# A two-layer conditioned transformer with routed experts, then a delta-rule block: where modulation, sums and paired weights are loaded

## The chip, the core and the metric

The kernel runs on one core of a Trainium2 chip, all in fp32. The metric is device time in microseconds (us) of one execution. Times come from runs of the whole kernel, the trace from one profiled execution.

## What is computed

Two layers of a first block are followed by one layer of a second block, on 512 tokens of width 1024 with 256 context tokens beside them in the first layer:

```python
mods = silu(c) @ ada_w[i] + ada_b[i]        # 6 x 1024: shift, scale, gate, twice; cmods from c_ctx
h = rms_norm(x, n1) * (1 + sc1) + sh1       # hc alike for the context
p = h @ w_in                                # 2304 columns: conv a, conv b, window and global attention
x_new = x + g1 * (concat(ya, yb, yc, yd) @ w_out)
h2 = rms_norm(x_new, n2) * (1 + sc2) + sh2
x_new = x_new + g2 * expert_choice_ffn(h2)  # 16 experts; each takes its best 64 tokens (32 of the context)
```

An expert computes `silu(xs @ w_gate) * (xs @ w_up) @ w_down` with three 1024 x 1024 matrices and adds its rows, times their gates, back to the tokens that it took. The second block (gated delta rule, dilated attention, a gated FFN) is not touched.

## The kernel before, in words

PE is TensorE, DVE VectorE, ACT ScalarE, POOL GpSimd; SP issues most loads. The program is written as one stream; a planner orders each engine's instructions by program order and a model of their times, so an instruction may stand earlier on its engine than in the program.

**Entry** (L213 to L399). SP loads the inputs: small parameter rows into `rows` (row_load, L223; five kinds of them on POOL's queue), four tiles of x, the first four 512-column blocks of layer 0's modulation weights (ada_load, L191: four loads of 512 KB a block), two tiles of context, and the first units of w_in (pre0). Blocks 0 and 1 are shift 1, blocks 2 and 3 scale 1. Each x tile is transposed by PE (L369), copied by ACT and scaled by DVE (L372). ada_gen (L309) multiplies a block with silu(c) (L318), copies the sums out (L323), transposes them (L327) and adds the bias on DVE (L329, L330). When all four blocks are done, norm1_first (L386) makes the eight 128-row blocks of the normalised input, as a rounded part `hh` (ACT, L396) and its rest `hl` (DVE L397, L398; POOL for the context). `dx` (L621, L622) stores the transposed x to DRAM and frees its place for the attention tiles; `tabl` (L638) loads the rotation tables there.

**Mixers and output product** (layer, L602). dense (L421) takes unit after unit of 128 output columns: a load of 512 KB into one of five `raw` tiles (raw_tile, L187), a split into `wh` (ACT, L442) and `wl` (POOL, L443), 24 matmuls over eight k blocks (L473, context L475), and an `ev` function. A unit of q gathers 64 + 64 columns from two places with two loads (colload2, L490), one unit for each j. Attention (L537), a 31-tap convolution (L773) and, in layer 0, modulation blocks 4 to 11 of layer 0 and 0 to 7 of layer 1 are woven into the dense steps (L943 to L947). The modulation loads use the same raw tiles. Then the output product runs with the router's logits (L974).

**Router and experts** (experts, L1022). Softmax and top-k run mainly on DVE (L1095 to L1180); the normalised tokens go to DRAM (`hd`, L1132), and gather (L1204) fetches an expert's tokens with an indirect DMA on POOL. wload (L1042) loads weight tiles of 512 KB in order of use: g0, u0, then for each expert g, d of the one before, u. In layer 0 the tiles are 18 `rawA`, five `raw` and two `rawB`; each product step (run_gu L1255, down L1324) pops one tile, multiplies it (L1243, context L1248; layer 1 L1237) and issues the next load. In layer 0, modulation blocks 8 to 11 of layer 1 are loaded through raw tiles ahead of the experts (L1061) and computed within the router's steps (L1090, L1120, L1150). There too, POOL clears a tile (L1136) and SP writes it over the sums (L1138). Experts add their output to `sumx` and `sumc` in DRAM with indirect DMAs (add_rows, L1299); near the end the sums come back through two tiles `rb` (sums_load L1305, after experts 13 and 14's up product), and PE and DVE turn and add them in twelve steps (sums_add, L1310): four within expert 15's up product, eight within its down product. The last experts' rows go through one-hot matmuls (scatter_x L1389, scatter_c L1417), with the squares of the new x for the next norm (L1401 to L1403).

```python
if 3 < b < 11 or (l == 1 and b != 7 and b < 11):       # L320, in ada_gen: prefetch the next block
    ada_load(l, b + 1, hfs=range(4 if l == 1 and b > 7 else 3))
run_all((dense_part(gd, 12), 12))                       # L943: the first four units
for e in range(17): ...                                 # L1443: g(e), down(e - 1), u(e), gather(e + 2)
```

## Time and profile before

| | us |
|---|---|
| runs | 2647.95, 2650.71, 2651.56 (median 2650.71) |
| profiled execution | 2657.17 |
| its span, first to last instruction | 2655.0 |
| its mean granted TensorE clock | 0.971 |

Layer 0's mixers and output product run from about 65 to 460 us, its router to 500, its experts to 1058; layer 1's mixers begin at 1083, its experts run from 1389 to 1860; the rest is the second block. A row of a timeline gives start, duration, engine, line, operation, tiles and, in brackets, how long the engine was idle before it and what ended that. "SPq" and "POOL ... DMA" rows are the issue of a transfer, not the transfer. A row with a count (x8) merges neighbours.

### The profile page before, as it was taken

The numbers are of one execution on the slowest core, as the hardware profiler recorded it, in microseconds if no ns is written. First come the engines' busy times: TensorE is split into PE (matmuls) and PEld (weight loads), VectorE is DVE, ScalarE is ACT, GpSimd is POOL, SyncE is SP. The second block draws the span as 40 slices with busy tenths as digits, with TensorE's granted clock in tenths as the row PEclk, the third lists the DMA queues.
The fourth block names the chain that finished last, engine by engine and source line by source line (L and its number), as shares of the span: only waits on it lengthen the run. The fifth ranks groups of instructions, "written<-read, shape, count | busy, mean of one in ns | idle before, by whom it ended". The sixth has DMA issues, their size and how long they took to land.

```text
span 2655.0 us, 41308 instructions
## 1 busy us (share of the span) xinstructions
PE 2476.4 (93%) x16415; PEld 1500.4 (57%) x16415; DVE 1092.9 (41%) x2371; ACT 870.2 (33%) x1769; POOL 637.8 (24%) x552
## 2 busy tenths in 40 slices
PE   7999999699999999899979989898899999999998
PEld 4766777344444333577753322132577787888886
DVE  4488852311111113689641102021665555444411
ACT  4544362211111110464531111110562435443422
POOL 3533112011111100633220000000333233444443
PEclk8999999899999999799989999999899999999999
DMA  8454455999999998222179999999421102333332
GB/s 281 140 165 139 149 177 197 322 383 385 385 386 385 388 394 313 58 59 52 61 289 386 394 398 399 399 404 409 130 67 32 40 25 64 95 96 96 92 96 67
DMA packets 324758, 584.08 MB, mean 220 GB/s; under 512 B 36864, under 2 KB 190007, under 8 KB 323927
## 3 DMA queue, kind: packets, MB, share of 16 engines
q1 hardware_dynamic: 311943, 555.16, 57.7%
q0 software_dynamic: 12480, 26.23, 4.1%
q8 instruction: 129, 2.11, 0.3%
q14 instruction: 62, 0.51, 0.1%
q10 hardware_dynamic: 144, 0.08, 0.0%
HBM read 556.74 MB, written 18.87 MB: 217 GB/s over the span
## 4 chain that ended last, share of the span: by engine, by line
PE 62%; DMA 21%; DVE 9%; issue 3%; POOL 2%; ACT 1%; SPq 1%; ACTq 0%; DVEq 0%; POOLq 0%
PE px L473 21%; DMA rawA<-in_w_gate_dram 4%; DMA rawA<-in_w_down_dram 4%; PE ax L1243 3%; DMA rawA<-in_w_up_dram 3%; PE yx L1243 3%; PE ux L1243 3%; PE g L473 2%; PE s L553 2%; PE y L584 2%; PE px L475 2%; DMA rawB<-in_w_gate_dram 2%; PE pt L565 2%; PE ac L1248 2%; PE pt L473 2%
## 5 line engine op out<-in xcount | busy, mean ns | idle before, releaser
L443 POOL TENSOR_TENSOR wl<-raw,wh 128x512 fp32r<-128x512 f32 (+1 forms) x312 | 408.2, 1311 | 962.0 <-ACT wh L442 768.1
L442 ACT ACTIVATE wh<-raw 128x512 fp32r<-128x512 f32 (+1 forms) x312 | 193.6, 625 | 441.2 <-PE px L473 211.0
L473 PE MATMUL px<-hh,wh 128*128 128x512 f32 x768 | 315.7, 412 | 6.4 <-DVE xT L1401 1.8
L473 PE MATMUL px<-hh,wl 128*128 128x512 f32 x768 | 313.1, 408 | 6.6 <-POOL wl L443 6.6
L473 PE MATMUL px<-hl,wh 128*128 128x512 f32 x768 | 314.6, 410 | 3.8 <-DVE hl L1019 1.9
L1225 ACT ACTIVATE xt<-tr,mod,a 128x64 f32<-128x64 f32 x256 | 86.9, 405 | 295.5 <-PE tr L1221 285.1
L473 PEld LDWEIGHTS px<-hh,wh 128*128 128x128 f32 x768 | 148.7, 194 | 41.2 <-issue 6.1
L473 PEld LDWEIGHTS px<-hh,wl 128*128 128x128 f32 x768 | 148.8, 194 | 39.7 <-POOL wl L443 7.3
L473 PEld LDWEIGHTS px<-hl,wh 128*128 128x128 f32 x768 | 148.7, 194 | 37.5 <-issue 3.8
L1369 DVE SCALAR_TENSOR_TENSOR Yx<-yx,gcol,Yx 64x512 fp32r<-64x512 f32 x36 | 27.0, 750 | 268.7 <-ACT Yx L1368 268.7
L1209 POOL DMA_INDIRECT xg<-hd,gidx x32 | 29.7, 927 | 431.9 <-PE tr L1221 398.3
L785 DVE SCALAR_TENSOR_TENSOR yT<-ub,cols,yT 128x512 f32<-128x512 f32 (+1 forms) x180 | 126.5, 718 | 0.6
L1243 PE MATMUL ax<-rawA,xt 128*32 128x512 f32 x856 | 116.8, 597 | 2.2 <-DMA rawA<-in_w_gate_dram 2.1
L1273 ACT ACTIVATE sa<-ax 128x512 f32<-128x512 f32 x32 | 19.1, 597 | 290.9 <-PE ax L1243 183.1
L1300 POOL DMA_INDIRECT sumx<-ys,place x14 | 22.0, 1571 | 376.5 <-ACT ys L1347 376.5
L1243 PE MATMUL ux<-rawA,xt 128*32 128x512 f32 x800 | 106.1, 594 | 0.1
L1237 PE MATMUL ux<-rawA,xt 128*64 128x512 f32 x328 | 87.3, 611 | 8.1 <-DMA rawA<-in_w_up_dram 8.0
L1237 PE MATMUL yx<-rawA,hT 128*64 128x512 f32 x316 | 81.5, 621 | 11.0 <-DMA rawA<-in_w_down_dram 10.0
L565 PE MATMUL pt<-tab,P 128*128 128x128 f32 x448 | 82.2, 284 | 6.8 <-DVE PT L571 4.3
L1368 ACT ACTIVATE Yx<-yx,gcol 64x512 fp32r<-64x512 f32 x36 | 24.6, 682 | 190.7 <-PE yx L1237 138.4
L1228 DVE TENSOR_SCALAR xt<-tr,a,mod 128x32 f32<-128x32 f32 x128 | 39.0, 310 | 115.0 <-ACT xt L1225 114.5
L1237 PE MATMUL ax<-rawA,xt 128*64 128x512 f32 x316 | 77.7, 612 | 7.6 <-DMA rawA<-in_w_gate_dram 7.2
(593 smaller groups left out, 4895.0 us busy)
## 6 DMA issues: line engine op xcount, KB each, us to landing
rawA<-in_w_gate_dram SPq DMA_DIRECT2D x186, 512.0 KB, 10.4
rawA<-in_w_up_dram SPq DMA_DIRECT2D x182, 512.0 KB, 10.2
rawA<-in_w_down_dram SPq DMA_DIRECT2D x151, 512.0 KB, 10.4
raw<-in_ada_w_dram SPq DMA_DIRECT2D x80, 512.0 KB, 5.7
raw<-in_w_down_dram SPq DMA_DIRECT2D x74, 512.0 KB, 10.2
raw<-in_w_gate_dram SPq DMA_DIRECT2D x62, 512.0 KB, 8.1
raw<-in_w_in_dram SPq DMA_DIRECT2D x56, 512.0 KB, 3.9
raw<-in_w_up_dram SPq DMA_DIRECT2D x55, 512.0 KB, 10.2
```

The source lines that it names most:

```text
L442: A.activation(wh[:, :n], raw[i][:, a:a + n], AF.Copy)
L443: G.tensor_tensor(wl[:, :n], raw[i][:, a:a + n], wh[:, :n].bitcast(F32), op=OP.subtract)
L473: T.matmul(px, lhsT=w[:, k % 4, :], rhs=h[:, k0 + k, 0:512], start=st, stop=sp_)
L475: T.matmul(pc, lhsT=w[:, k % 4, :], rhs=h[:, k0 + k, 512:nt], start=st, stop=sp_)
L553: T.matmul(s[:, :w], lhsT=q, rhs=k, start=(a == 0), stop=(a == len(mm) - 1))
L565: T.transpose(pt[:, (t - a) * 128:(t - a + 1) * 128], P[:, t * 128:(t + 1) * 128], ident)
L584: T.matmul(y[64 * g:64 * g + 64, bi * 128:(bi + 1) * 128], lhsT=vs[g][t], rhs=PTs[i, g][t // 4][:, (t % 4) * 128:(t % 4 + 1) * 128], start ...
L785: V.scalar_tensor_tensor(acc[:, j, o:o + n], src, w, acc[:, j, o:o + n], op0=OP.mult, op1=OP.add)
L1225: A.activation(xt[:, kk, 0:64], p[:, k * NX:k * NX + 64], AF.Identity, bias=M[l][:, 24 + kk, 0:1], scale=a2[:, kk, 0:1])
L1237: T.matmul(px[64 * g:64 * g + 64, :], lhsT=lx(u), rhs=w[:, 512 * hf:512 * hf + 512], start=first, stop=last)
L1243: T.matmul(px[32 * g:32 * g + 32, :], lhsT=lx(u)[:, 32 * (g % 2):32 * (g % 2) + 32], rhs=w[:, 512 * hf:512 * hf + 512], start=first, stop= ...
L1248: T.matmul(pc[32 * g:32 * g + 32, :], lhsT=lc(u), rhs=w[:, 256 * q:256 * q + 256], start=first, stop=last)
```

## The change

- The entry loads all of x first, then modulation blocks 0 and 2, the context, the first unit of w_in, blocks 1 and 3, and the first q pair; small rows follow, all on SP, and `rows` lies in a raw tile. `pre0[2]` is loaded too.
- Blocks 0 and 2 alone are computed ahead of the first four blocks of the normalised input; blocks 1 and 3 come after the first half of the first dense unit. The three remaining transposes of rows move behind the first unit.
- A q pair's two units share two loads of 512 KB with 256 columns each (pair_load).
- Layer 1's modulation blocks 8 to 11 become 16 more units at the end of layer 0's list of expert loads, in `rawA` tiles, and are computed step by step within scatter_x.
- The sums are cleared beside the output product, from part of `lg`.
- The sums are added back one product earlier: the context's in expert 14's up product (loaded after expert 12's), four steps in expert 15's up product, four in its down product.
- Within the loop over experts SP's instructions keep the order of the program, in both layers.

```diff
@@ tiles and entry @@
-    dx = pool(ctx, "dx", space=DRAM).tile([128, 8 * 768], F32)
+    dxp = pool(ctx, "dx", space=DRAM)
+    dx = dxp.tile([128, 8 * 768], F32)
+    accs = dxp.tile([1024, 512], F32, name="sumx"), dxp.tile([1024, 256], F32, name="sumc")
...
-    rows = ent.tile([128, 4, 128], F32)
+    rows = raw_tile()[:, 0:512].rearrange("p (g c) -> p g c", g=4)
...
-    ada0 = ent.tile([128, 4, 4, 1024], F32)
+    entry2 = ExitStack()
+    ada0 = {b: pl.tile([128, 4, 1024], F32, name=f"ada{b}")
+            for pl, bs in ((ent, (1, 3)), (pool(entry2, "ent2", side="right"), (0, 2))) for b in bs}
...
-    x_load(1)
-    row_load(G, 0, "qn", I["q_norm_g"], 2, dup=True)
-    row_load(G, 0, "kn", I["k_norm_g"], 2, dup=True)
-    row_load(G, 0, "cbb", I["conv_b_b"].rearrange("l (h p) -> (l h) p", p=128), 4)
...
+    for t in range(1, 4):
+        x_load(t)
+    ada_load(0, 0, ada0[0])
+    ada_load(0, 2, ada0[2])
+    for t in range(2):
+        SY.dma_start(cin[:, t, :], I["ctx"][0, t * 128:(t + 1) * 128, :])
+    pre0 = {0: raw_tile().rearrange("p (k c) -> p k c", k=8)}
+    SY.dma_start(pre0[0], I["w_in"][0, :, 1536:1664].rearrange("(k p) c -> p k c", p=128))
+    ada_load(0, 1, ada0[1])
+    ada_load(0, 3, ada0[3])
+
+    def pair_load(src, c0):
+
+        ts = [raw_tile(), raw_tile()]
+        for i, t in enumerate(ts):
+            SY.dma_start(t.rearrange("p (k c) -> p k c", k=4),
+                         src[512 * i:512 * i + 512, c0:c0 + 256].rearrange("(k p) c -> p k c", p=128))
+        return ts
+
+    pre0[1] = pre0[2] = pair_load(I["w_in"][0], 1280)
+    row_load(SY, 0, "qn", I["q_norm_g"], 2, dup=True)
+    row_load(SY, 0, "kn", I["k_norm_g"], 2, dup=True)
...
-    x_load(2)
...
-    x_load(3)
...
-    ada_load(0, 0, ada0[:, 0], hfs=(0, 1))
...
-    ada_load(0, 0, ada0[:, 0], hfs=(2, 3))
-    ada_load(0, 2, ada0[:, 2])
-    for t in range(2):
-        SY.dma_start(cin[:, t, :], I["ctx"][0, t * 128:(t + 1) * 128, :])
-    ada_load(0, 1, ada0[:, 1])
...
-    pre0[1] = raw_tile().rearrange("p (k c) -> p k c", k=8)
-    for h in range(2):
-        SY.dma_start(pre0[1][:, :, 64 * h:64 * h + 64],
-                     I["w_in"][0, :, 1280 + 128 * h:1344 + 128 * h].rearrange("(k p) c -> p k c", p=128))
-    ada_load(0, 3, ada0[:, 3])
@@ ada_gen @@
-            if 3 < b < 11 or (l == 1 and b != 7 and b < 11):
-                ada_load(l, b + 1, hfs=range(4 if l == 1 and b > 7 else 3))
+            if 3 < b < 11 and l == 0 or l == 1 and b < 7:
+                ada_load(l, b + 1, hfs=range(3))
@@ entry block @@
-            ga = ada_gen(0, (0, 2, 1, 3), sqp, pse)
+            ga = ada_gen(0, (0, 2), sqp, pse)
...
-            for g in (0, 2, 3):
-                rows_to_cols(g, RO["n", g])
-            V.tensor_scalar(nsink, sinkb, -1.0, None, op0=OP.mult)
-
-        entry.close()
-
-        def norm1_first(sqp):
-            a1 = sqp.tile([128, 8, 2], F32, name="a1")
-            for k in range(8):
+
+        entry2.close()
+
+        def norm1_first(ks, a1):
+            for k in ks:
@@ dense @@
+                elif i < len(units) and len(units[i]) == 6 and units[i][5]:
+                    raw[i] = raw[i - 1]
+                elif i < len(units) and len(units[i]) == 6:
+                    raw[i] = units[i][0]()
...
-                        A.activation(wh[:, :n], raw[i][:, a:a + n], AF.Copy)
-                        G.tensor_tensor(wl[:, :n], raw[i][:, a:a + n], wh[:, :n].bitcast(F32), op=OP.subtract)
+                        if len(units[i]) == 6:
+                            src = raw[i][a // 4].rearrange("p (q j c) -> p q j c", j=2, c=64)[:, :, units[i][5], :]
+                            wh_, wl_ = (w.rearrange("p k (h c) -> p (k h) c", h=2) for w in (wh, wl))
+                        else:
+                            src, wh_, wl_ = raw[i][:, a:a + n], wh[:, :n], wl[:, :n]
+                        A.activation(wh_, src, AF.Copy)
+                        G.tensor_tensor(wl_, src, wh_.bitcast(F32), op=OP.subtract)
@@ layer @@
-                    norm1_first(sqp)
+                    a1 = cst.tile([128, 8, 2], F32)
+                    norm1_first(range(4), a1)
+                    gd = dense(units, hh, hl, dw, psp, pre=pre0, ahead=4)
+                    next(gd)
+                    drain(ada_gen(0, (1, 3), sqp, psp))
+                    norm1_first(range(4, 8), a1)
+                    entry.close()
                     xip_es.close()
...
-                run_all((dense_part(gd, 12), 12))
+                if has:
+                    for _ in range(2):
+                        next(gd)
+                    for g in (0, 2, 3):
+                        rows_to_cols(psp, "misc", g, RO["n", g])
+                    V.tensor_scalar(nsink, sinkb, -1.0, None, op0=OP.mult)
+                run_all((dense_part(gd, 9 if has else 12), 12))
...
+                    G.memset(lg[:, 0:512], 0.0)
+                    for acc_, n in zip(accs, (8, 4)):
+                        SY.dma_start(acc_.rearrange("(p a) c -> p (a c)", p=128).rearrange("p (b c) -> p b c", c=512),
+                                     lg[:, None, 0:512].to_broadcast([128, n, 512]))
@@ experts @@
+            if has:
+                units += [("ada", b, hf) for b in range(8, 12) for hf in range(4)]
...
-                    k = slots[i % len(slots)]
+                    k = slots[i % len(slots)] if w != "ada" else "A"
...
-                    SY.dma_start(r, W[w][l, e, 128 * u:128 * u + 128, :])
-                    wt[w, e, u] = r
+                    if w == "ada":
+                        SY.dma_start(r.rearrange("p (k c) -> p k c", k=2),
+                                     I["ada_w"][1, u * 256:u * 256 + 256, e * 512:e * 512 + 512]
+                                     .rearrange("(k p) c -> p k c", p=128))
+                        raws["ada", 1, e, u] = r
+                    else:
+                        SY.dma_start(r, W[w][l, e, 128 * u:128 * u + 128, :])
+                        wt[w, e, u] = r
...
-            if has:
-                ada_load(1, 8)
...
-                    ga = ada_gen(1, range(8, 12), mp, Psum(ps, {"yx": 1}, {"misc": "yx"})) if has else iter(())
...
-                    for _ in steps(ga, 2):
-                        pass
...
-                        G.memset(zz, 0.0)
-                        for acc_, n in zip(accs, (512, 256)):
...
-                        if i in (2, 4, 6):
-                            for _ in steps(ga, 2):
-                                pass
...
-                            each(8 + u // 2)
+                            each(u)
...
-                        if has and e == 15:
-                            sums_add(u)
+                        if has and e == 15 and u % 2:
+                            sums_add(4 + u // 2)
...
                         if last and has:
+                            next(ga)
...
+                with tc.manual_schedule(engines={mybir.EngineType.SP}):
...
-                        if has and e == 15:
-                            run_gu("u", e, [], sums_add)
+                            if has and e == 15:
+                                run_gu("u", e, [], lambda u: sums_add(u // 2))
+                            elif has and e == 14:
+                                run_gu("u", e, mid, lambda u: sums_add(8 + u // 2))
...
-                        if has and e in (13, 14):
-                            for t in ((4, 5), range(4))[e - 13]:
+                            if has and e in (12, 14):
+                                for t in ((4, 5), range(4))[e // 2 - 6]:
                                     sums_load(t)
...
+                    ga = ada_gen(1, range(8, 12), Psum(sp, {"ys": None}, {"sq": "ys"}), Psum(ps, {"ux": 1}, {"misc": "ux"}))
```

## Rows read from the trace of the kernel before

**Rows 1.** The page, busy time of each engine over the span.

```profile
PE 2476.4 (93%) x16415; PEld 1500.4 (57%) x16415; DVE 1092.9 (41%) x2371; ACT 870.2 (33%) x1769; POOL 637.8 (24%) x552
```

**Rows 2.** Busy time by stretches: us, each engine's busy us, PE clock, DMA share, GB/s.

```profile
20.00:40.00 20.00, 12.97 (x72) 4.55 (x66) 4.71 (x12) 7.95 (x16) 3.29 (x3) 1.00 0.98 330
...
480.00:500.00 20.00, 4.50 (x12) 1.11 (x13) 8.00 (x44) 0.00 (x0) 1.93 (x2) 0.52 0.92 302
...
800.00:850.00 50.00, 50.00 (x614) 20.51 (x610) 6.16 (x16) 5.92 (x14) 5.07 (x4) 1.00 1.03 393
...
1060.00:1080.00 20.00, 15.22 (x41) 9.15 (x41) 16.12 (x33) 11.33 (x22) 9.82 (x8) 0.52 0.08 31
```

**Rows 3.** Timeline of the entry.

```profile
24.78 9.45 SPq L272 DMA_DIRECT2D raw<-in_w_in_dram  x2
...
37.34 0.51 SPq L621 DMA_DIRECT2D dx<-xT  x1
...
42.84 3.35 PE L318 MATMUL misc<-ada,s 128*32 128x512 f32 x8 [0.40 <-DMA ada<-in_ada_w_dram]
...
49.41 0.79 PE L473 MATMUL px<-hh,wh 128*128 128x512 f32 x1 [1.41 <-ACT hh L396]
...
63.81 0.68 DVE L398 TENSOR_TENSOR hl<-xin,hh 128x512 fp32r<-128x512 f32 x1
...
71.71 1.28 POOL L678 TENSOR_TENSOR sq<-sq,tabl 128x512 f32<-128x512 f32 x1 [2.21 <-DMA tabl<-in_tab_dram]
```

**Rows 4.** Timeline of the router in layer 0, and three rows of layer 1.

```profile
457.98 0.59 PE L974 MATMUL s<-xcT,rs 128*32 128x256 f32 x2
...
462.30 1.93 PE L318 MATMUL yx<-raw,s 128*32 128x512 f32 x16
...
464.97 0.66 PE L327 MATMUL yx<-tab,sq 128*128 128x128 f32 x4 [0.74 <-ACT sq L323]
...
479.36 0.60 SPq L1138 DMA_DIRECT2D sumx<-ht  x1
...
485.02 1.00 POOL L1209 DMA_INDIRECT xg<-hd,gidx  x1 [6.65 <-DVE tA L1191]
...
496.26 3.44 PE L318 MATMUL yx<-raw,s 128*32 128x512 f32 x8 [14.04 <-DMA raw<-in_ada_w_dram]
...
499.63 1.06 PE L1221 MATMUL tr<-tab,xg 96*128 96x96 f32 x5
...
1360.46 1.96 PE L974 MATMUL s<-xT,rs 128*32 128x512 f32 x8
...
1384.05 1.24 POOL L1209 DMA_INDIRECT xg<-hd,gidx  x1 [22.89 <-DVE tA L1191]
...
1388.26 1.08 PE L1221 MATMUL tr<-tab,xg 64*128 64x64 f32 x8 [6.38 <-DMA xg<-hd,gidx]
```

**Rows 5.** DVE's product after layer 0's experts 0, 10 and 15 (sixteen such).

```profile
530.75 0.69 DVE L1281 TENSOR_TENSOR sa<-ux,sa 128x512 f32<-128x512 f32 x1 [1.77 <-PE ux L1243]
...
859.25 0.69 DVE L1281 TENSOR_TENSOR sa<-ux,sa 128x512 f32<-128x512 f32 x1 [1.76 <-PE ux L1243]
...
1037.72 0.69 DVE L1281 TENSOR_TENSOR sa<-ux,sa 128x512 f32<-128x512 f32 x1 [5.32 <-PE ux L1243]
```

**Rows 6.** Timeline of the end of layer 0.

```profile
1051.57 0.63 PE L1317 MATMUL tr<-tab,rb 128*128 128x128 f32 x4 [2.11 <-DMA rb<-sumx]
...
1057.58 0.66 PE L1317 MATMUL tr<-tab,rb 128*128 128x128 f32 x4
...
1064.00 9.40 POOL L287 TENSOR_TENSOR stA<-stA,sq 128x512 f32<-128x512 f32 x7 [4.48 <-ACT sq L286]
...
1083.39 0.80 PE L473 MATMUL px<-hh,wh 128*128 128x512 f32 x1 [1.17 <-ACT hh L416]
```

**Rows 7.** SP's own waits: what for, us in total, times, longest us.

```profile
SPq L487 <- POOL wl L443: 850.2, 99, 38.4
```

**Rows 8.** The page, DMA issues: count, KB each, us to landing.

```profile
raw<-in_w_in_dram SPq DMA_DIRECT2D x56, 512.0 KB, 3.9
```

More of the change, by code (lines that the diff above doesn't have):

```diff
@@ L332, in ada_gen, with rows_to_cols @@
             yield
+    def rows_to_cols(psp, name, g, n):
+        p = psp.tile([128, 512], F32, name=name)
+        T.transpose(p[:, :n], rows[0:n, g, :], ident[0:n, 0:n])
+        V.tensor_copy(cols[:, g, 0:n], p[:, :n])
     es_l0 = ExitStack()
@@ L345, in main_kernel @@
             pse = Psum(ep, {"tp": 4, "misc": 2, "rb": 1, "rc": 1})
-            def rows_to_cols(g, n):
-                p = pse.tile([128, 512], F32, name="rc")
-                T.transpose(p[:, :n], rows[0:n, g, :], ident[0:n, 0:n])
-                V.tensor_copy(cols[:, g, 0:n], p[:, :n])
-            rows_to_cols(0, 16)
+            rows_to_cols(pse, "rc", 0, 16)
             A.activation(s2[:, :, 0], col("c"), AF.Silu)
             A.activation(s2[:, :, 1], col("cc"), AF.Silu)
-            ga = ada_gen(0, (0, 2, 1, 3), sqp, pse)
+            ga = ada_gen(0, (0, 2), sqp, pse)
             ss = ent.tile([128, 6], F32)
@@ L615, in layer @@
                 psp = Psum(ps, {"px": 3, "s": 2, "pt": 1, "misc": 1, "y": 1}, {"pc": "px"})
+                c0 = dict(a_b=0, a_c=256, a_h=512, b_v=768, b_g=1024, c_q=1280, c_k=1536, c_v=1664,
+                          d_q=1792, d_k=2048, d_v=2176)
+                evs = []
+                units = []
+                for n in "c_k c_q c_v b_g b_v d_k d_q d_v a_c a_h a_b".split():
+                    for j in range(2 if n[2] == "q" or n[0] in "ab" else 1):
+                        nt, ev = NT if n[2] == "q" or n[0] in "ab" else 768, partial(lambda i, px, pc: evs[i](px, pc), len(units))
+                        if n[2] == "q":
+                            units.append((partial(pair_load, w_in, c0[n]), ev, nt, 0, 8, j))
+                        else:
+                            units.append((colload(w_in, c0[n] + 128 * j), ev, nt))
                 if has:
                     hh, hl = hh0, hl0
-                    norm1_first(sqp)
+                    a1 = cst.tile([128, 8, 2], F32)
[5 more added lines that the diff above has]
+                    entry.close()
                     xip_es.close()
@@ L931, in rest @@
                     yield
-                ga = iter(())
                 if has:
@@ L938, in layer @@
                     ga = ada_rest()
-                gd = dense(u_c + u_b + u_d + u_a, hh, hl, dw, psp, pre=pre0 if has else {}, ahead=4 if has else None)
+                else:
+                    ga = iter(())
+                if not has:
+                    gd = dense(units, hh, hl, dw, psp)
                 at, cv = att_gen(), conv31()
                 w1, w2, w3 = (28, 28, 64) if has else (18, 18, 44)
-                run_all((dense_part(gd, 12), 12))
+                if has:
[5 more added lines that the diff above has]
+                run_all((dense_part(gd, 9 if has else 12), 12))
                 run_all((dense_part(gd, 12), 12), (steps(at, w1), w1), (steps(ga, 8), 8))
@@ L1067, in experts @@
                 if has:
-                    accs = dr.tile([1024, 512], F32, name="sumx"), dr.tile([1024, 256], F32, name="sumc")
                     place = mp.tile([128, 2, 16], I32)
```

81 lines of the change are left out of this document (31 added, 50 removed).

## Prediction, before the changed kernel was run

> **What bounds the kernel now.** I read the page first, then the busy time by stretches, then the timeline around every edit, and the chain of waits to see which waits are on the path. TensorE (PE) is busy 93% of the span in that view [rows 1], so time is to be won only where PE stands still, or where it does work that could lie elsewhere. The stretches show where that is: in the entry DMA runs at only 330 GB/s, the router's stretch 480 to 500 has 4.50 us of PE in 20, and 1060 to 1080 has PE at clock 0.52 [rows 2]. In the first layer's experts (800 to 850) PE is busy throughout while DMA is full too, at 393 GB/s [rows 2]. Both are near their limits there, so a start moved earlier carries through to the end of the stage only if both move.
>
> The profiled execution took 2657.2 us, 6.5 above the median of 2650.7. The sum below is a difference, which I take from both.
>
> **Entry.** Before, the two half-width loads of pre0[1] keep SP issuing for 9.45 us; the last modulation matmuls wait for DMA until 42.84; the first dense matmul is at 49.41, and the eighth block of normalised input is ready at 63.81 + 0.68 = 64.5 [rows 3]. After, what stands ahead of ada block 3's end is x 2.1, four ada blocks 8.4, ctx 1.05, one w_in unit 0.52 and small rows, some 12.2 MB. At 375 GB/s (between the 330 of this stretch and the 393 of the stream) that takes 32.5 us, from the start at 3: 35.5, with 34 and 40 as ends. Before, that data was complete between the matmuls' start at 42.84 and their end at 46.19, which I put at 44: 8.5 earlier. The eight blocks took 64.5 - 49.4 = 15.1 us on DVE; now four of them, with half of the first unit's matmuls, run on blocks 0 and 2 while 1 and 3 still land, so 7.5 remain behind: 16 won in all. Against it: the two dx stores (3.1 MB, 8 us at 393 GB/s) were issued at 37.34, ahead of need, and now stand behind 18 small loads on SP (seven of them taken from POOL's queue, where they had cost nothing). The table load on POOL must wait until the stores have freed its place, and POOL already waited 2.21 us for it [rows 3]: 2.5 back. The three row transposes, 1 us, move onto PE's path behind the first unit. **Minus 12.5, between minus 5 and minus 18.** The paired loads of the other q units lie beside dense work in stages where PE waits for no weight load: nothing, unless they come late (last rival).
>
> **Router.** The zeroing of the sums (3.1 MB) is issued on SP from 479.36, late ada loads follow it, and the first gather goes out among them at 485.02; PE first waits 14.04 us for an ada load, does its matmuls, and the first expert transpose comes at 499.63, 14.6 after the gather's issue. In layer 1, with neither, it comes 4.2 after (1384.05 to 1388.26) [rows 4]. With both gone I take 5: minus 9.5. If the seven weight loads that no longer queue behind ada tiles meet the gather (3.7 MB, 9.4 us at 393 GB/s) only 6 is won; the other end is 10.4. From the last logits matmul to the gather's issue is 26.5 us (457.98 + 0.59 to 485.02) against 21.6 in layer 1 (1360.46 + 1.96 to 1384.05) [rows 4]; the modulation's work on PE, ACT and DVE goes from between, and layer 0 keeps six token tiles against four: minus 2.5, between 0 and minus 4.8.
>
> **First expert.** From 499.63 to the first `sa` product at 530.75 is 31.1 us. In the steady stretch an expert takes (859.25 - 530.75) / 10 = 32.85 us, and two of its three products with the transposes 21.9 [rows 5]. The other 9.2 is late modulation, in PE's order. Minus 9; at least two blocks of 1.93 + 0.66 [rows 4], 5.2.
>
> **The stream.** Layer 0's five raw tiles no longer hold ada blocks, so all 25 tiles of weights can be filled before the gather, and the loads behind them start as much earlier as PE does. So the lead of DMA over PE is at least the old one. From 859.25 to 1037.72 PE took 178.5 us for five experts where the steady pace gives 164.3 [rows 5]: 14 lost to late weights and to transposes spread among products. I leave that loss as it is: 0, between minus 10 and plus 5. Program order of the loads itself costs and gives nothing: nearly everywhere SP already issues gate, down, up in the order of use. Layer 1's stage is bound by the same stream and only starts earlier.
>
> On the bandwidth of that stream the row shows 393 GB/s. The Trainium skill (DMA: Bandwidth & Descriptors, Specifications) gives about 358 GB/s as what HBM grants a core; 359 units of 0.524 MB would then need 526 us where the row's rate needs 479, and the stream alone would end the stage. The trace does not agree, so this gets no chance.
>
> **Sums.** From 1037.72 to the last sums transpose at 1057.58 + 0.66 is 20.5 us for the last down product, with a 2.11 wait for a sums load [rows 5, 6]. After, one third of an expert (10.9) and four groups of transposes of 0.66 (2.6) remain, 13.5; the four others go to the up product before (plus 2.6), and those of the context one up product earlier. The loads go out earlier on POOL, behind adds that have landed by then. Minus 4, between 0 and minus 7. Zeroing: one memset on POOL (about 1 us) and two stores of 8 us on SP, ahead of the w_out loads, while two units are already in: nothing; if that cover fails, up to 8.
>
> **Late blocks in the tail.** Four blocks of 1.93 + 0.66 are 10.4 us of PE work [rows 4], now between the output scatter's matmuls, in a stretch that ran from 1058 to the next dense matmul at 1083.39 and whose slowest engine was POOL with 9.40 us of adds [rows 6]. PE was busy 15.2 of 20 there [rows 2], so about half fits in the gaps: plus 5. The ends are 0 and plus 12, the upper one when the blocks run at the clock that this stretch had, 0.52, which is the 1.2 GHz level: 7.7 more for four blocks. The loads, 8.4 MB or 21 us, follow the last weight while sums are still being added, so I take them as landed in time.
>
> The Trainium skill (TensorE: Matmul & The Clock Gate, Part 1) has an idle array at the lower clock and sustained work releasing it; by that rule the added matmuls could themselves bring the clock back, and the tail would cost 5, not 12. The row can't tell, since it has no such work in it.
>
> **Sum:** -12.5 - 9.5 - 2.5 - 9 + 0 - 4 + 5 = -32.5. The profiled execution would be 2624.7, the median 2618. All ends together give -59 and +1. What a measurement of this kernel can tell from no change is about 0.2%, 5.3 us.
>
> **Rivals.**
> 1. *The late blocks stall the tail.* Their last loads wait for rawA tiles that the last down product frees, and PE works in order: one matmul waiting for a block holds the scatter behind it, as one held the router for 14 us [rows 4]. Against it: DMA has nothing else to do by then. Tail +20 instead of +5: 2633. Chance 0.14.
> 2. *The entry's gain is swallowed* by the dx stores behind the small loads, and by the table that all rotations need: entry 4 instead of 12.5, 2627. For it, the 2.21 wait [rows 3]; against it, the modulation blocks really land 8.5 us earlier. Chance 0.12.
> 3. *The stream takes back the router's gain.* If DMA sets the end of layer 0's experts, the 21 won by gather, top-k and first expert go into later waits for weights, and only entry, sums and tail remain (-12.5 - 4 + 5): 2639. For it, the 14 us lost late; against it, the loads start earlier as well. Chance 0.06.
> 4. *Slower: the mixers starve.* Place: the pool of five raw tiles. A pair takes two tiles at once and gives both back only after its second unit is split, and at first the rows sit in a tile, so the next load waits longer on SP, and those behind it too. SP waits 850.2 us in 99 cases for the split already, and a w_in load lands in 3.9 us [rows 7, 8]. Some 31 loads of the two mixers are so placed; each that becomes exposed costs 3.9, so nine eat the 32.5, and beyond that the change is slower. With 15 exposed: 2618 + 58 = 2676. Against it: with units of 9 us, a load of 3.9 has slack. Chance 0.08.
>
> **Numbers.** The forecast holds 0.60. Rivals 1 to 3 are faster too, except for an edge of 0.04 near no change. Faster 0.88, same 0.04, slower 0.08. The range goes from 2594 (nearly all favourable ends) to 2645 (past rivals 1 to 3).
>
> **What would show it.** Right: first dense matmul near 30 and the end of the first unit 12 to 15 us earlier; no L318 wait in the router and about 5 us from gather to first transpose; first `sa` some 22 us after that; both sums stores beside w_out; the last down product in about 14 us; L318 in the scatter at the end of layer 0. Wrong: a long wait of PE for an ada load in the tail, waits of POOL for the table above 5 us, dense matmuls waiting for w_in, or an expert pace above 36 us early in layer 0.

## The result and the profile after

| | runs | median, us | lowest to highest, us |
|---|---|---|---|
| before | 4 | 2651.14 | 2647.95 to 2656.49 |
| after | 4 | 2616.09 | 2608.99 to 2617.45 |

The ratio is 0.986, 95% interval 0.9836 to 0.9885: 35 us faster, where 2618 and 32.5 us had been forecast. The profiled execution after took 2617.36 (span 2615.6, clock 0.980); against the profiled one before that is 39.8, because that one stood above its median.

The page after, busy time of each engine, answers [rows 1]: the same matmuls, 33 us less of them busy and 39 less span.

```profile
PE 2443.3 (93%) x16415; PEld 1487.9 (57%) x16415; DVE 1095.3 (42%) x2371; ACT 869.6 (33%) x1769; POOL 631.5 (24%) x545
```

Busy time by stretches after (columns as in [rows 2]): the entry is fuller, the stretch at 480 is now dense expert work, the steady stream is as before, and the end of layer 0 runs at clock 0.98, where it had 0.52.

```profile
20.00:40.00 20.00, 14.91 (x75) 6.48 (x72) 11.00 (x24) 12.07 (x23) 6.78 (x6) 0.91 1.01 343
480.00:500.00 20.00, 20.00 (x248) 7.82 (x244) 3.30 (x11) 5.66 (x13) 0.90 (x1) 1.00 0.96 343
800.00:850.00 50.00, 50.00 (x608) 20.60 (x604) 5.97 (x15) 5.23 (x13) 4.06 (x3) 1.00 1.03 390
1019.70:1047.60 27.90, 23.93 (x131) 10.33 (x130) 21.67 (x50) 16.60 (x33) 14.77 (x13) 0.98 0.72 236
```

Timeline of the entry after, answering [rows 3]. The first dense matmul comes 15.9 us sooner. The last block of input is made at 53.3 instead of 64.5, which is 11.2: block 3's sum (DVE L337) waits until 44.1 for PE, since the planner put most of the first half of the unit ahead of block 3's last matmuls. The table, behind the dx stores, still holds POOL, and through it PE.

```profile
33.54 0.50 PE L486 MATMUL px<-hh,wh 128*128 128x512 f32 x1
41.44 1.06 PE L326 MATMUL misc<-ada,s 128*32 128x512 f32 x8
44.10 0.19 DVE L337 TENSOR_REDUCE mod<-misc 128x8 f32<-128x32 f32 x1 [7.65 <-PE misc L335]
45.41 0.51 SPq L647 DMA_DIRECT2D dx<-xT  x1
52.62 0.68 DVE L402 TENSOR_TENSOR hl<-xin,hh 128x512 fp32r<-128x512 f32 x1
60.71 1.26 POOL L704 TENSOR_TENSOR sq<-sq,tabl 128x512 f32<-128x512 f32 x1 [1.75 <-DMA tabl<-in_tab_dram]
63.70 0.79 PE L486 MATMUL px<-hh,wl 128*128 128x512 f32 x1 [2.36 <-POOL wl L456]
```

Timeline of the router after, answering [rows 4]: the last logits matmul, the gather's issue, and the first expert transpose, which now waits for the gather and for nothing else, 4.5 us behind its issue.

```profile
446.21 0.59 PE L996 MATMUL s<-xcT,rs 128*32 128x256 f32 x2
471.82 0.98 POOL L1228 DMA_INDIRECT xg<-hd,gidx  x1 [25.34 <-DVE tA L1210]
476.34 1.51 PE L1240 MATMUL tr<-tab,xg 96*128 96x96 f32 x8 [7.38 <-DMA xg<-hd,gidx]
```

Timeline after: the products with `sa` of experts 0, 10 and 15, as in [rows 5], and the end of layer 0, as in [rows 6]. The late blocks (L326) start right behind the last sums transpose.

```profile
500.09 0.69 DVE L1300 TENSOR_TENSOR sa<-ux,sa 128x512 f32<-128x512 f32 x1 [1.79 <-DMA rawA<-in_w_up_dram]
828.58 0.69 DVE L1300 TENSOR_TENSOR sa<-ux,sa 128x512 f32<-128x512 f32 x1 [1.77 <-PE ux L1262]
1003.67 0.69 DVE L1300 TENSOR_TENSOR sa<-ux,sa 128x512 f32<-128x512 f32 x1 [1.19 <-PE ux L1262]
...
1019.07 0.66 PE L1336 MATMUL tr<-tab,rb 128*128 128x128 f32 x4
1019.66 1.90 PE L326 MATMUL ux<-rawA,s 128*32 128x512 f32 x10
...
1047.64 0.80 PE L486 MATMUL px<-hh,wh 128*128 128x512 f32 x1 [0.91 <-ACT hh L420]
```

From these rows, each step's change is a difference of two intervals:

| stretch | before | after | change | forecast |
|---|---|---|---|---|
| start to the end of the logits | 458.57 | 446.80 | -11.8 | -12.5 |
| to the gather's issue | 26.45 | 25.02 | -1.4 | -2.5 |
| to the first expert transpose | 14.61 | 4.52 | -10.1 | -9.5 |
| to the first `sa` product | 31.12 | 23.75 | -7.4 | -9 |
| to the last `sa` product of layer 0 | 506.97 | 503.58 | -3.4 | 0 |
| to the end of the last sums transpose | 20.52 | 16.06 | -4.5 | -4 |
| to layer 1's first dense matmul | 25.15 | 27.91 | +2.8 | +5 |
| to the end of the span | 1571.6 | 1568.0 | -3.6 | 0 |

The forecast's lines add up to -32.5. The last line is not of the change: a second profile of the same kernel (the base run below) has 1570.6 there. Without that line the sum is -35.8.

### The profile page after: what moved, and what is told of

Same layout as the page of the kernel before. It is cut to its first block, busy times and chain, and to the rows that moved or that the text cites. A ratio compares the mean times of both kernels' runs of the same rounds, so it can differ in the third digit from the quotient of the medians.

```text
span 2615.6 us, 41294 instructions
## 1 busy us (share of the span) xinstructions
PE 2443.3 (93%) x16415; PEld 1487.9 (57%) x16415; DVE 1095.3 (42%) x2371; ACT 869.6 (33%) x1769; POOL 631.5 (24%) x545
## 4 chain that ended last, share of the span: by engine, by line
PE 65%; DMA 20%; DVE 9%; POOL 2%; issue 2%; ACT 2%; SPq 0%; ACTq 0%; DVEq 0%; POOLq 0%
PE px L486 21%; DMA rawA<-in_w_down_dram 5%; DMA rawA<-in_w_gate_dram 4%; PE yx L1262 4%; PE ax L1262 4%; PE ux L1262 3%; DMA rawA<-in_w_up_dram 3%; PE g L486 2%; PE y L591 2%; PE s L560 2%; PE px L488 2%; PE yc L1267 2%; PE ac L1267 2%; DMA rawB<-in_w_gate_dram 2%; PE pt L572 2%
## 5 line engine op out<-in xcount | busy, mean ns | idle before, releaser
L486 PEld LDWEIGHTS px<-hh,wh 128*128 128x128 f32 x768 | 146.8, 191 | 41.4 <-issue 7.1
L486 PEld LDWEIGHTS px<-hh,wl 128*128 128x128 f32 x768 | 147.0, 191 | 39.8 <-POOL wl L456 7.9
L1370 DVE TENSOR_SCALAR yt<-yc,gcol 128x256 f32<-128x256 f32 x12 | 5.8, 484 | 178.1 <-PE yc L1267 178.1
```

Source lines behind the costliest of these rows:

```text
L486: T.matmul(px, lhsT=w[:, k % 4, :], rhs=h[:, k0 + k, 0:512], start=st, stop=sp_)
```

## The experiments

Runs that were taken together share a chip and its runs of the kernel before, whose medians lay between 2651 and 2656 from one such group to the next; the changed kernel's two medians differ by 0.4. Two profiles of the changed kernel differ by 3 us from 33.5 to the first modulation matmul of the mixers alone (93.23 and 90.29). So parts are priced by medians against 2616.3, the mean of the changed kernel's two medians, and profiles tell where the time lies. The changed kernel's eight runs lie between 2608.99 and 2617.45, and the runs without late blocks, with planned loads, with dx sooner and with both edits overlap that range, so these prices aren't told from nothing by the runs alone.

| run | median, us | against the changed kernel | ratio to before, 95% interval |
|---|---|---|---|
| after, again | 2616.49 | 0 | 0.9863 (0.9838 to 0.9888) |
| entry as before | 2629.01 | +12.7 | 0.9910 (0.9894 to 0.9926) |
| zeroing in the router | 2622.07 | +5.8 | 0.9880 (0.9862 to 0.9897) |
| late blocks in the router | 2639.23 | +22.9 | 0.9941 (0.9926 to 0.9957) |
| no late blocks | 2610.68 | -5.6 | 0.9841 (0.9822 to 0.9859) |
| sums as before | 2622.29 | +6.0 | 0.9883 (0.9858 to 0.9909) |
| planned loads | 2615.36 | -0.9 | 0.9860 (0.9835 to 0.9885) |
| entry alone, on the kernel before | 2640.04 | +23.7 | 0.9946 (0.9932 to 0.9959) |
| dx sooner, blocks 1 and 3 sooner | 2619.76 | +3.5 | 0.9874 (0.9846 to 0.9902) |
| blocks 1 and 3 first | 2621.31 | +5.0 | 0.9877 (0.9861 to 0.9893) |
| both | 2613.83, again 2615.06 | -2.5, -1.2 | 0.9855 (0.9837 to 0.9873), 0.9843 (0.9823 to 0.9863) |

Landmarks of one profile each (us; starts of the instructions, the logits and the sums transposes by their end):

| | logits | gather | transpose | first sa | eleventh sa | last sa | last sums | dense, layer 1 |
|---|---|---|---|---|---|---|---|---|
| before | 458.57 | 485.02 | 499.63 | 530.75 | 859.25 | 1037.72 | 1058.24 | 1083.39 |
| after | 446.80 | 471.82 | 476.34 | 500.09 | 828.58 | 1003.67 | 1019.73 | 1047.64 |
| after, again | 444.53 | 468.14 | 472.61 | 496.69 | 825.17 | 998.86 | 1014.92 | 1043.74 |
| entry as before | 452.12 | 475.65 | 479.88 | 503.82 | 832.31 | 1006.69 | 1022.75 | 1050.67 |
| zeroing in the router | 447.42 | 470.90 | 477.80 | 502.65 | 831.14 | 1006.08 | 1022.14 | 1050.08 |
| late blocks in the router | 451.04 | 479.17 | 485.06 | 516.60 | 845.09 | 1029.21 | 1044.69 | 1069.81 |
| no late blocks | 447.87 | 471.49 | 476.14 | 500.31 | 828.79 | 1002.71 | 1018.78 | 1043.89 |
| sums as before | 448.21 | 471.82 | 476.20 | 500.38 | 828.86 | 1002.08 | 1022.80 | 1051.21 |
| entry alone | 448.81 | 475.96 | 490.79 | 521.50 | 849.99 | 1028.13 | 1046.56 | 1071.68 |

**The base, and the entry.**

> The changed kernel itself once more, as the base for the other runs of the same chip: some 36 us faster than before; single profiles of one and the same entry code differed by 6 us at the end of the first mixers, so differences below that are read from medians alone.

```diff
-            ga = ada_gen(0, (0, 2), sqp, pse)       # and the order of loads, rows, pairs: all as before
+            ga = ada_gen(0, (0, 2, 1, 3), sqp, pse)
...
-                    norm1_first(range(4), a1)
-                    gd = dense(units, hh, hl, dw, psp, pre=pre0, ahead=4)
...
+                    norm1_first(sqp)
```

> The changed kernel with its entry (order of the first loads, four modulation blocks ahead of the first dense product, paired loads) as it was before; all the rest is the change. Theory (what the entry wins is kept to the end): the router starts 11.8 us later than in the changed kernel, everything behind it moves by the same, so about 12 us slower than the changed kernel: some 23 us faster than before, near 2628. Rival (the first layer's experts are bound by the weight stream, which starts with w_out and takes part of it back; or the dx stores swallow it): 4 us or less slower than the changed kernel, near 2620.

It was 12.7 slower, as the theory says. Its own profile, of an execution 3.8 us below the run's median, shows just 5.3 of it at the logits (452.12), and yet up to there PE runs the program of the kernel before, whose profile has 458.57. These 6.5 us lie between two executions: 2.5 of them stand at the first dense matmul already (46.94 in this run, 49.41 before), and 1.6 around the end of the mixers, where PE never idles and its clock is 0.94 in this run and 0.88 before. So the price rests on the medians. The complement, the kernel before with the entry's part alone:

```diff
+            ga = ada_gen(0, (0, 2), sqp, pse)       # the entry and the pairs of the change, on the kernel before
...
+                    norm1_first(range(4), a1)
+                    gd = dense(units, hh, hl, dw, psp, pre=pre0, ahead=4)
...
```

> The kernel before with the entry's part of the change alone (order of the first loads, modulation blocks 1 and 3 behind the first dense matmuls, paired loads); router, zeroing, late blocks and sums stay as before. Theory (the parts add up): taking the entry back cost the changed kernel 10 to 13 us, so the entry alone wins 10 to 13: near 2640, and the run without the late blocks' move, 15.8 faster than before, is the entry plus next to nothing for the zeroing and the sums. Rival (the entry's gain survives only with the freed router behind it): less than 6 us faster than before.

It won 14.8 against its runs of before (10.9 to 18.1 by the interval). From both sides the entry, with the pairs, is worth 12 to 15, and the gain is kept with either kernel behind it.

**The zeroing.**

```diff
-                    G.memset(lg[:, 0:512], 0.0)              # beside the output product, with its two stores
...
+                    if has:                                  # behind the token stores, in the router
+                        zz = sqp.tile([128, 1024], F32, name="ht", bufs=4)
+                        G.memset(zz, 0.0)
...
```

> The changed kernel with one edit undone: the memset and the two stores that zero the sums stand in the router again, behind the token stores. Late modulation stays behind the stream. Theory A (the zeroing's 3.1 MB alone is what made the gather late): from the gather's issue to the first expert transpose 10 us or more instead of 4.5, and the kernel 5 to 8 us slower than the changed one, near 2623. Theory B (the late modulation loads and their place in PE's order made it, the zeroing only shares the engines): 4.5 to 7 us, and the kernel at most 2 us slower, near 2617.

Between the theories, B's wait and A's price: the first transpose comes 6.9 us behind the gather's issue instead of 4.5. From the logits to the last `sa` it is 558.7 us, where the two profiles of the changed kernel have 556.9 and 554.3; the medians say 5.8. With zeroing and no late blocks, the gather alone is the wait (timeline of the router, this run):

```profile
465.15 0.60 SPq L1162 DMA_DIRECT2D sumx<-ht  x1
470.90 0.98 POOL L1230 DMA_INDIRECT xg<-hd,gidx  x1 [6.77 <-DVE tA L1212]
477.80 1.51 PE L1242 MATMUL tr<-tab,xg 96*128 96x96 f32 x8 [9.68 <-DMA xg<-hd,gidx]
```

**The late blocks.**

```diff
-                units += [("ada", b, hf) for b in range(8, 12) for hf in range(4)]
+            if has:
+                ada_load(1, 8)
...
+                    ga = ada_gen(1, range(8, 12), mp, Psum(ps, {"yx": 1}, {"misc": "yx"})) if has else iter(())
...
+                        if i in (2, 4, 6):
+                            for _ in steps(ga, 2):
+                                pass
```

> The changed kernel with the four late modulation blocks of the second layer back in the raw tiles, the router and the first expert, as before; the zeroing stays beside w_out. Theory of the forecast: the router and the first expert lose 9 + 2.5 us and part of the 9.5, the scatter at the end of layer 0 wins back 2.8 to 5: first up product's product with sa some 13 to 17 us later than in the changed kernel, the kernel 8 to 14 us slower, 2624 to 2630. Rival (the stream sets the end of these experts and takes a router's gain back): the last sa of layer 0 is less than 4 us later than in the changed kernel, and the kernel is within 3 us of it.

It lost 22.9, more than either said, though the first `sa` comes 16.5 later, as the theory had it. The landmarks, as differences to the changed kernel's intervals, place it: the output product 4.2 (383.63 to 448.76 instead of 444.52), logits to gather 3.1, gather to transpose 1.4, first expert 7.8, the last five experts 9.0; the last down product and the scatter give back 0.6 and 2.8. Two of these had no price in the forecast. The 4.2 stand in the output product: in this run only two of its loads stand on SP ahead of the zeroing, since three of the five raw tiles hold the first loads of block 8; in the changed kernel five do. The third goes out behind the zeroing's stores and is split at 392.85. In the entry alone, with the same two loads and no zeroing there, it is split at 385.50, and these eight units take 60.8 us, as in the changed kernel (60.9; here 65.1). Timeline of SP and of that split, this run, then SP in the changed kernel:

```profile
356.15 1.04 SPq L500 DMA_DIRECT2D raw<-in_w_out_dram  x2
...
369.81 0.60 SPq L1023 DMA_DIRECT2D sumx<-lg  x1
370.46 0.67 SPq L1023 DMA_DIRECT2D sumc<-lg  x1
371.23 10.61 SPq L500 DMA_DIRECT2D raw<-in_w_out_dram  x2
...
392.85 1.66 ACT L455 ACTIVATE wh<-raw 128x512 fp32r<-128x512 f32 x3
```

```profile
347.02 13.32 SPq L500 DMA_DIRECT2D raw<-in_w_out_dram  x5
...
371.33 0.60 SPq L1023 DMA_DIRECT2D sumx<-lg  x1
```

The 9.0 stand in the last five experts, and little of them is late weights. Every kernel here keeps 32.85 us an expert for ten experts or more. Then, in this run, experts 12 to 15 take 36.2, 36.7, 40.1 and 38.2 us; in the changed kernel 33.9, 37.7, 35.8 and 34.8. Both have the 2.6 us of moved transposes in expert 14. The timeline of the products with `sa` in this run, the last three:

```profile
950.84 0.69 DVE L1305 TENSOR_TENSOR sa<-ux,sa 128x512 f32<-128x512 f32 x1 [7.12 <-PE ux L1267]
990.96 0.69 DVE L1305 TENSOR_TENSOR sa<-ux,sa 128x512 f32<-128x512 f32 x1 [2.48 <-PE ux L1267]
1029.21 0.69 DVE L1305 TENSOR_TENSOR sa<-ux,sa 128x512 f32<-128x512 f32 x1 [5.32 <-PE ux L1267]
```

What differs is PE's order. In this run the transposes of experts 12 to 15 stand mostly one or two at a time between the steps on weight tiles (80 in 53 groups), in the changed kernel four to eight together (76 in 14 groups). PE's timeline in expert 14, this run, then the changed kernel:

```profile
983.76 1.07 PE L1267 MATMUL ux<-raw,xt 128*32 128x512 f32 x8
...
985.19 0.33 PE L1341 MATMUL tr<-tab,rb 128*128 128x128 f32 x1
985.45 1.06 PE L1267 MATMUL ux<-rawB,xt 128*32 128x512 f32 x8
...
988.56 1.04 PE L1267 MATMUL ux<-rawA,xt 128*32 128x512 f32 x8
...
989.85 1.04 PE L1267 MATMUL ux<-rawA,xt 128*32 128x512 f32 x8
```

```profile
956.14 1.04 PE L1262 MATMUL ux<-raw,xt 128*32 128x512 f32 x8
...
957.55 0.66 PE L1336 MATMUL tr<-tab,rb 128*128 128x128 f32 x4
958.13 1.06 PE L1262 MATMUL ux<-raw,xt 128*32 128x512 f32 x8
```

A step on one weight tile takes 1.29 us from start to start (988.56 to 989.85), with one transpose behind it 1.69, with two 1.80 (980.28 to 982.08), with four 1.99. Expert 14 of this run has 24 steps, twelve single transposes and nine pairs: 24 x 1.29 + 12 x 0.40 + 9 x 0.51 = 40.4, where 40.1 were measured, without one wait of PE above 0.15 us. In expert 15 PE has the same order, instruction by instruction, in this run, in the entry alone and in the kernel before, and it takes 38.25 in all three. The waits of PE that a weight load ends come to 2.7 us here and 3.4 in the changed kernel. So most of the 9.0 is the order that the planner makes with the late blocks in the raw tiles; why it makes that one isn't shown.

Set beside the entry alone, this run has zeroing and sums moved as well. It is 4.9 sooner at the first `sa`, still 4.1 after expert 13, and 1.1 later at the last: 5.2 go in expert 14, where its order holds the 2.6 of moved transposes. That isn't rival 3, which had the gain go into waits for weights. A gain at the head is kept elsewhere too: the entry alone has 9.3 at the first `sa` and 9.6 at the last against the kernel before; the entry as before loses 3.7 and 3.0 against the changed kernel.

**The blocks' price in the scatter.** Here blocks 8 to 11 of layer 1's modulation are left out and set to zero.

```diff
-                units += [("ada", b, hf) for b in range(8, 12) for hf in range(4)]
...
-                            next(ga)
...
+    V.memset(M[1][:, 32:48, :], 0.0)
...
```

> The changed kernel without the four late modulation blocks: their loads, matmuls, transposes and sums are left out (these columns of the modulation are set to zero once at the start). It prices the blocks in the scatter. Theory of the forecast: they cost 5, so this runs 5 us faster than the changed kernel, near 2611, with TensorE at clock 0.8 or more in the scatter. Rival (the clock): without them the stretch from the last sums transpose to the first dense matmul falls back to the clock it had before, 0.52, the scatter's own matmuls get longer, and the blocks cost nothing on balance: within 2 us of the changed kernel, with this stretch no shorter than its 27.9 us by more than 3.

By medians the blocks cost 5.6, but the five runs (2609.19 to 2617.10) lie in the changed kernel's range, and their mean is only 3.0 below its mean. From the last sums transpose to the dense matmul the profile shows 2.8 (27.9 against 25.1; 3.7 against the base run), and behind it nothing is won (1570.0 to the end, where the changed kernel's profiles have 1568.0 and 1570.6). So about 3 is shown. Of the theory the price came by medians, and the clock didn't: 0.65 in the stretch, not 0.8 or more. The rival's clock came nearly (0.52 was said); that the blocks cost nothing isn't what the stretch shows. Busy time of the stretch, this run:

```profile
1018.80:1043.90 25.10, 16.60 (x51) 10.58 (x51) 19.72 (x42) 14.44 (x29) 14.05 (x13) 0.65 0.10 32
```

The changed kernel has 131 matmuls and clock 0.98 there, the base run 0.93, before 0.55 in that stretch. A merged row of scatter matmuls of this run, and one of the changed kernel: 0.59 us each at the 1.2 GHz level, 0.30 at 2.4.

```profile
1023.79 5.89 PE L1415 MATMUL tr<-oh,Yx 128*128 128x512 f32 x10 [0.44 <-DVE xT L1418]
```

```profile
1028.37 1.20 PE L1417 MATMUL tr<-oh,Yx 128*128 128x512 f32 x4
```

So four blocks of 2.6 us lengthened the stretch by about 3: the gaps held some, and the scatter's own matmuls got shorter at the clock that came with the blocks. That is what the Trainium skill (TensorE: Matmul & The Clock Gate, Part 1) has, that activity releases the throttle; the trace agrees, 0.98 against 0.65.

**Sums and program order.**

```diff
-                        if has and e == 15 and u % 2:
-                            sums_add(4 + u // 2)
+                        if has and e == 15:
+                            sums_add(u)
...
-                            if has and e in (12, 14):
+                            if has and e in (13, 14):
```

> The changed kernel with the sums' transposes and loads back where they were: the context's four in the up product of expert 15, all eight of the tokens in the last down product, their loads after experts 13 and 14. Theory of the forecast: the work is the same, but it stands in the tail, and one load is late again: from the last sa product to the last sums transpose 20 us instead of 16.1, the kernel 4 us slower. Rival (the late weights set the end of the up product of expert 15 whatever stands between, so sums taken out of there free time that is waited away): the last sa 2 to 3 us earlier, and the kernel within 2 us of the changed one.

6.0 slower: the theory, with 20.7 us in the last down product (1002.08 to 1022.80). Of the rival's 2 to 3 us little came (from the eleventh `sa` to the last 173.2 us instead of 175.1 and 173.7): expert 14 falls back to 32.85, but expert 15 takes 37.0 instead of 34.8, as the context's transposes stand one or two at a time there. One transpose waits for its sums load again:

```profile
1015.95 0.63 PE L1336 MATMUL tr<-tab,rb 128*128 128x128 f32 x4 [1.38 <-DMA rb<-sumx]
```

```diff
-                with tc.manual_schedule(engines={mybir.EngineType.SP}):
+                if True:
```

> The changed kernel without the one edit that keeps SP's loads in program order in the experts, so the planner orders them in both layers. Theory of the forecast (SP already issues them in the order of use nearly everywhere): within 3 us of the changed kernel. Rival (program order is what lets the weights come in time late in layer 0, where the loss went from 14 to 10.8): the pace of experts 12 to 16 is worse by 3 us or more in layer 0, and layer 1 by some more: 4 to 8 us slower.

The same time to within what can be told (0.9 less). The rival falls: late in layer 0 its pace is no worse (172.8 us from the eleventh `sa` to the last, where the changed kernel has 175.1 and 173.7), nor is what follows (1569.3 from layer 1's first dense matmul to the end, against 1568.0 and 1570.6).

**Beyond the change.** Three edits of the entry go after the wait that the profile after shows.

```diff
-                    drain(ada_gen(0, (1, 3), sqp, psp))      # behind next(gd)
+                    drain(ada_gen(0, (1, 3), sqp, Psum(ps, psp.bufs, {"misc": "s"})))   # ahead of it
...
+        SY.dma_start(dx[:, 0:4096], xT.rearrange("p k c -> p (k c)"))    # ahead of the small row loads
```

> Beyond the change: modulation blocks 1 and 3 stand ahead of the first dense product in the program with two accumulators instead of one, and the dx stores go out ahead of the small row loads. In the changed kernel the second half of block 3's matmuls stands at 41.44, behind 5 us of dense matmuls, while VectorE idles from 36.5 to 44.1 for it; the table load waits for dx and POOL and PE for the table. Theory (this order, not the data, now sets the end of the first unit): the last block of input at 49 instead of 53.3, no 2.4 us wait of PE for a split near 63, and the kernel 4 to 6 us faster than the changed one. Rival (the data of block 3 lands only then, or the dx stores take its bandwidth): the matmuls wait for a load, and nothing is won.

Nothing was won (+3.5, with ranges that overlap). The planner still set dense matmuls ahead of block 3's last ones; the sum came at 42.6.

```diff
-                    gd = dense(units, hh, hl, dw, psp, pre=pre0, ahead=4)
-                    next(gd)
-                    drain(ada_gen(0, (1, 3), sqp, psp))
+                    with tc.manual_schedule(engines={mybir.EngineType.PE}):
+                        drain(ada_gen(0, (1, 3), sqp, Psum(ps, psp.bufs, {"misc": "s"})))
+                        gd = dense(units, hh, hl, dw, psp, pre=pre0, ahead=4)
+                        next(gd)
```

> Beyond the change, PE's order fixed by hand at one place: modulation blocks 1 and 3 with their transposes, in two accumulators, all ahead of the first dense matmul; the loads stay as they are. In the run before this one the planner still put a dense matmul that waits for POOL ahead of block 3's last matmuls (the sum came at 42.6 instead of 44.1). Theory: block 3's data is there by 33, its sum at 37, the last block of input at 46 to 48 instead of 53.9; but the table, behind the dx stores of 45.4, comes no sooner than at 60, so of 6 to 8 us half is kept: 2612 to 2614. Rival (the table alone sets the first units' end): nothing is won, 2616.

5.0 slower by medians, near the edge of the intervals; in any case nothing won, and the rival's wait is there. The data isn't there by 33: the last load ends a wait at 38.27, so the sum can't come before 41, and the dense matmuls now stand behind it (first at 40.43). What is won for the last block of input goes into a longer wait for the table (2.98 instead of 1.75). Timeline of this run:

```profile
38.27 1.05 PE L326 MATMUL s<-ada,s 128*32 128x512 f32 x4 [0.27 <-DMA ada<-in_ada_w_dram]
40.71 0.19 DVE L337 TENSOR_REDUCE mod<-s 128x8 f32<-128x32 f32 x1 [3.13 <-PE s L335]
60.63 1.29 POOL L705 TENSOR_TENSOR sq<-sq,tabl 128x512 f32<-128x512 f32 x1 [2.98 <-DMA tabl<-in_tab_dram]
```

With the dx stores ahead of the row loads as well (the two diffs together):

> The run with the blocks first, and the dx stores ahead of the small row loads on SP too. Theory (blocks and table both set the first units): 6 to 8 us faster than the changed kernel, near 2609, with the table landed by 54. Rival (the row loads and w_in loads behind dx come late, as SP was busy with them to 51.7 in the run that moved dx): no faster than with the blocks first alone.

> The run with modulation blocks 1 and 3 first and the dx stores ahead of the row loads once more, since its median of 2613.83 stands only 2.3 to 2.7 us from the changed kernel's two medians (2616.09 and 2616.49). If it is faster by what its profile shows (the first units' end 3 to 5 us sooner), the median is again at 2614 or below and 40 us or more under before; if it is the same kernel to within what can be told, the median lies between 2614 and 2618.

POOL's wait for the table is gone (timeline of the first of these):

```profile
57.01 1.30 POOL L704 TENSOR_TENSOR sq<-sq,tabl 128x512 f32<-128x512 f32 x1
```

The medians lie 2.5 and 1.2 below the changed kernel's, within the intervals: not told from it. The second time the two signs disagree: 2615.06 is where the same kernel was to lie, but 41.4 under its own runs of before is what a faster one was to show. The 6 to 8 us of the theory were not there; half of them hung on data that lands at 38.

## Why the prediction was right, point by point

- **Entry, -12.5.** Right by the runs (12 to 15). Inside it, data was put at 35.5 and came near 38 (38.27 in the run with the blocks first), within its ends, and the saving behind it was cut by the planner's place for block 3: the last block of input comes 11.2 sooner, where 16 were reckoned. The first dense matmul came at 33.5, not 30, and the first unit's sums are read 10 us sooner (55.68 instead of 65.66), not 12 to 15. The 2.5 for the table don't show: PE waits 2.36 for the split behind it, where it waited 2.14 before.
- **Router, -21.** The three terms came to 18.9 in the profile, with the gather slightly better and the first expert at 23.75 instead of 21.9. But the reasons don't add as the working had it. Late blocks and zeroing together make 14.6 us, and the entry alone still has 14.8; either alone leaves 5.9 or 6.9. The gather itself shows it: the first one lands 4.4 us after its issue with neither, 5.8 with the late blocks, 6.8 with the zeroing, and 10.0 with both. So of the 14.6 some 10 were the gather; the late load ended PE's wait 1.2 us behind its landing, and its matmuls took the rest.
- **Zeroing at nothing, "while two units are already in".** The result holds and the premise doesn't: with two units in, the output product loses 4.2 us, inside the "up to 8" of the failed cover. It was free because five were in, which the late blocks' move out of the raw tiles made room for.
- **The stream, 0.** Mis-sized: 3.4 shorter although 2.6 us of transposes were moved into it, 6 in all. The forecast named late weights and transposes spread among products as what 14 us were lost to, and left both as they were. The waits for weights didn't shrink (2.1 us in the kernel before, 3.4 after), but with the late blocks out of the raw tiles the planner puts the transposes together (64 in 41 groups before, 76 in 14 after, experts 12 to 15). It is PE's order that got better, not the stream.
- **Sums, -4.** The last down product took 16.1, not 13.5, since the turn of `sa` into `hT`, 2.8 us from 1003.67 to the first down matmul, was left out of the sum. The run with the edit undone takes 222.4 us from the eleventh `sa` to layer 1's first dense matmul, where the changed kernel has 219.1 and 218.6: 3.3 to 3.8, and 6.0 by medians.
- **Tail, +5.** 2.8 to 3.7 in the profile, 5.6 by medians that can't be told from it; between the ends, and without rival 1's stall, since no late matmul waits for a load there.
- **Program order and pairs.** Nothing for the first (-0.9). The pairs were not tried by themselves. Matmuls take w_in through its split, so rival 4's place is ACT's wait for w_in in layer 0's mixers (65 to 460 us): 22.7 us in six cases, where the kernel before has 23.0 in six; and PE waits for no split there. In the entry, ACT's split of the second unit waits 5.1 us for it once, at 39.4, while PE has the first.
- The figure of about 358 GB/s of the Trainium skill (DMA: Bandwidth & Descriptors, Specifications) got no chance, rightly: the stream after runs at 390 GB/s at 800 to 850, where it had 393.

## What to carry to other kernels

A load that an in-order engine must wait for can cost what its queue has in front of it (14.0 us behind 3.1 MB of stores and late loads here), so move the load or the backlog, and expect that the two moves are not worth the sum of their prices. Work that nobody needs yet belongs behind a long stage and not into its start: the four late blocks moved there were worth some 20 us, of which 12 lay in the router and the first expert and 9 showed up over 300 us later, in the last experts. Where a planner orders an engine, moving a block in the program need not move it on the engine, and can reorder other work far behind it: read the order after.

## What the runs showed of the hardware that was not expected

- Profiles of one and the same program differ by 3 to 6 us over entry and mixers. Part of it is the clock: 188 matmuls around the end of the mixers, with PE never idle, took 29.66 us at a granted clock of 0.88 in the kernel before and 28.10 at 0.94 in the run with the old entry. Part of it is waits: the two profiles of the changed kernel have 10.9 and 8.5 us of idle PE between the first dense matmul and the first modulation matmul of the mixers.
- Four blocks of PE work, 10.4 us, added to a stretch that ran at clock 0.55 to 0.65 lengthened it by about 3 us: PE was busy for only 16.6 of its 25.1 us without them, and the whole stretch then ran at 0.93 to 0.98.
- At 390 GB/s, with DMA full all along, PE keeps 32.85 us an expert to within 0.01 for eleven experts, and a shortage of weights shows only from expert 12 on. SP's issues in the trace show the lead going: at the first `sa` it has issued 24 weight tiles more than PE has used, at the twelfth 9. When the tiles landed isn't shown, as the trace has no landing of these loads.
- A transpose that stands alone between two steps on weight tiles lengthened PE's sequence by 0.40 us, four together by 0.70, with no wait in either.
